# Sparse-attention scores over 128 contraction rows, shared keys projected feature-major, compression with two stacked parts

## The chip, the core and the metric

The kernel runs on one core of a Trainium2 chip. The core has five engines with an instruction queue each: TensorE (PE in the profile; its weight loads are listed as PEld), VectorE (DVE), ScalarE (ACT), GpSimd (POOL) and SyncE (SP), which here only issues weight loads from HBM. Products go from SBUF through PE into PSUM banks of 128 partitions by 512 float32, and ACT and DVE read them from there. The metric is the device time of one execution in microseconds (us), from the start of the program to its end; lower is better.

## The reference

Two transformer blocks on 256 tokens of width 1024, all in float32. The first block (gated mix of three attentions, feed-forward) is not touched. The second has two layers: feed-forward, a spatial gating unit, feed-forward; then feed-forward, a native sparse attention (NSA), feed-forward. Keys and values of the sparse attention are made from the activations that enter the second layer (`kv`, six slots of 4 groups by 64 features):

```python
kv = (h @ kv_w).reshape(B, S, N_KV_SLOTS, N_KV_GROUPS, HEAD_DIM_2)
k_cmp = compress(kv[:, :, 0], cmp_pe[0], cmp_w1[0], cmp_b1[0], cmp_w2[0])
v_cmp = compress(kv[:, :, 1], cmp_pe[1], cmp_w1[1], cmp_b1[1], cmp_w2[1])
# slots 2, 3: keys and values of the selected blocks; slots 4, 5: of the window
...
def compress(kv, pe, w1, b1, w2):      # 15 blocks of 32 tokens, stride 16, per group
    ...
    return jax.nn.gelu(flat @ w1 + b1, approximate=False) @ w2      # flat: 2048 wide, w1: 2048 x 256
```

With 256 tokens every selected block lies inside the causal range, so selection and window both come down to causal attention of 16 heads over all earlier tokens, once with the keys of slot 2 and values of slot 3, once with slots 4 and 5, with a bias by distance; the compressed branch adds attention over the 15 compressed keys and values.

## The kernel before, in words

**Precision.** PE multiplies float32 exactly only in four slow passes. So most operands are kept as two float32r parts, high and low (`wh`, `wl` of a weight; two `big` tiles of activations), and a product is three matmuls: high by high, high by low, low by high (`mm3`, L273 to L275). In the profile such a matmul shows as L273, L274 or L275, whoever called it. `up` (weights stationary, all 256 tokens moving, output feature-major, two tiles of 128 features by 256 tokens in a bank) takes 48 matmuls of 256 columns per chunk of weights; `row` (activations stationary, weights moving, output token-major) takes 24 matmuls per 128 tokens, of as many columns as the weights have.

**Weights.** `Stream` loads them in the order of use, in half chunks of 512 KB (5 raw buffers `wr`), splits each with a cast on ACT (L140) and a subtraction on DVE (L147), and holds four chunks of split weights. Every `W.get` takes the next chunk and prepares those that follow.

**The stage that is changed, `kv_ffn` (L985).** It runs the projection of `kv` ahead of the first feed-forward of the second layer and hides its small work in that feed-forward: the generator `ff` loops over chunks `c` of 256 hidden features (two `up`, the activation, then the product into the accumulators, `down`, L309) and calls `hooks[c]` on the way.
- The projection is token-major: three chunks of 512 columns, each for two tiles of 128 tokens (`row`, 24 matmuls of 512 columns). ACT copies the results from PSUM into `kvc` (slots 0 and 1, L996), `ks` (keys, L998) and `self.v` (values, L999).
- `heads_T` (L1019) turns a slot feature-major: DVE duplicates each group's 64 features side by side (L1024), PE transposes (8 per slot, L1029), so each group lies on both halves of the partitions. The hook `keys` (c = 1) does so for slots 2 and 4 and splits them into `self.kh` and `self.kl`; the hooks `windows(0)` and `windows(1)` (c = 2, 3) do so for slots 0 and 1, one half shifted by a token (L1059 on ACT, L1060 on DVE), add the position term (L1070) and split the result.
- The hook `compress` (c = 4, L1074) multiplies, for each of two slots, 60 blocks (15 by 4 groups) by `w1` in 16 steps of 128 rows with `mm3`: 48 matmuls with 60 stationary columns and 256 moving ones. DVE copies the result (L1085), PE transposes it in two pieces (L1089, 60 rows), ACT applies the gelu (L1091), and products with `w2` follow (L1097; L1112 after eight DVE copies, L1106).

**The scores, in `nsa` (L1123).** `stack` puts the queries of a head into `Q` with the high part on one half of the partitions and the low part on the other. For each of 4 heads, 4 groups and 2 token tiles `score` writes a bank with two matmuls: `Q[:, j]` by `kh` over all 128 rows (L1273: high and low query by the high key), then the high half `Q[a, j]` by the same half of `kl` (L1274: 64 rows). Both move `2 * nk` columns: 256 for the first token tile, 512 for the second. `attention` (L635) runs groups of heads in a pipeline: scores two groups ahead of the transposes (L667), those one ahead of the products with the values (L681); DVE adds the mask and takes the minimum (L657), ACT applies exp (L659).

**What sets the order.** A list scheduler of the tile framework orders each engine's instructions when the kernel is built; each engine then runs its own list strictly in order, and semaphores hold it where an operand or buffer is not ready. Weight loads stand in the order of `Stream`.

## Time and profile before

| what | value |
|---|---|
| three runs, median (lowest to highest) | 1521.57 us (1514.3 to 1526.19) |
| span of the profiled execution, first to last instruction | 1511.4 us |
| PE busy | 1469.7 us, 97% of the span, 9817 matmuls |
| DVE busy | 955.1 us, 63% |
| ACT busy | 745.9 us, 49% |
| POOL busy | 64.9 us, 4% |
| granted TensorE clock, mean | 0.995 |
| read from HBM | 262.09 MB, 174 GB/s over the span |

The span lies 10.2 us under the median and 2.9 us under the fastest of the three runs; what lies around the first and last instruction is in the runs' times and not in the span. Matmuls are pipelined, so the length of one in the profile (0.28 us for 256 columns, 0.39 us for 512) is not what it costs a busy PE: that is the distance from its start to the start of the next, called a slot here.

### The profile page before, as it was taken

What the parts mean: (1) busy time and instruction counts of PE and PEld (TensorE: products, weight loads), DVE (VectorE), ACT (ScalarE), POOL (GpSimd) and SP (SyncE); (2) the same over time, 40 slices, a digit from 0 to 9 for tenths busy, and PEclk for the clock granted to TensorE, in tenths of its full rate; (3) what the DMA queues carried; (4) which work ended last, traced back from release to release, by engine and by line L of the source; (5) the groups of instructions that cost most, each with busy time, mean ns of one, the idle gap of its engine ahead of it and who ended that gap; (6) DMA issues with size and microseconds to landing.
All of it is one profiled execution on the core that took longest, in us unless ns stands there. A gap on an engine that the chain in (4) does not pass through costs nothing.

```text
span 1511.4 us, 24692 instructions
## 1 busy us (share of the span) xinstructions
PE 1469.7 (97%) x9817; PEld 1323.7 (88%) x9817; DVE 955.1 (63%) x1611; ACT 745.9 (49%) x1141; POOL 64.9 (4%) x79
## 2 busy tenths in 40 slices
PE   7999999999999999999999999999999999999997
PEld 6798987989889999799889999799999787899996
DVE  7884388555584555876774455767655777765545
ACT  5565554444454443544454443545544486444442
POOL 0000030000000000100010000100000121100002
PEclk9999999999999999999999999999999999999999
DMA  8352266655646556576556655555765442275550
GB/s 283 116 181 88 77 232 223 210 184 185 190 168 189 186 184 194 171 206 245 173 173 190 191 185 182 168 176 188 255 186 182 145 141 65 70 242 189 184 181 28
DMA packets 188640, 264.78 MB, mean 175 GB/s; under 512 B 11024, under 2 KB 153708, under 8 KB 188524
## 3 DMA queue, kind: packets, MB, share of 16 engines
q1 hardware_dynamic: 179996, 249.56, 51.5%
q10 hardware_dynamic: 8528, 13.64, 3.0%
q8 instruction: 77, 1.26, 0.3%
q14 instruction: 39, 0.32, 0.1%
HBM read 262.09 MB, written 1.07 MB: 174 GB/s over the span
## 4 chain that ended last, share of the span: by engine, by line
PE 76%; DVE 6%; DMA 1%; ACT 1%; issue 0%; POOL 0%; DVEq 0%; ACTq 0%; SPq 0%
PE acc L309 21%; PE u L273 15%; PE u L275 15%; PE u L274 15%; DVE big L836 1%; PE acc L681 1%; PE acc L273 1%; PE acc L275 1%; PE acc L274 1%; DVE bst L366 1%; DVE big L813 1%; PE u L1274 1%; PE acc L667 1%; DMA wr<-in_ffn_w_dram 1%; DVE nwa L335 1%; DMA wr<-in_w_mlp_out_dram 1%
## 5 line engine op out<-in xcount | busy, mean ns | idle before, releaser
L147 DVE TENSOR_TENSOR wl<-wr,wh 128x1024 fp32r<-128x1024 f32 (+4 forms) x488 | 577.1, 1191 | 447.0 <-ACT wh L140 443.2
L140 ACT CAST wh<-wr 128x1024 fp32r<-128x1024 f32 (+4 forms) x488 | 494.2, 1019 | 545.1 <-PE u L274 240.2
L273 PE MATMUL u<-big,wh 128*128 128x256 f32 x1896 | 534.1, 282 | 1.1 <-ACT med L399 0.9
L275 PE MATMUL u<-big,wl 128*128 128x256 f32 x1896 | 532.0, 281 | 0.0
L274 PE MATMUL u<-big,wh 128*128 128x256 f32 x1896 | 531.9, 281 | 0.0
L273 PEld LDWEIGHTS u<-big,wh 128*128 128x128 f32 x1896 | 356.9, 188 | 4.7 <-ACT med L399 1.1
L274 PEld LDWEIGHTS u<-big,wh 128*128 128x128 f32 x1896 | 356.4, 188 | 2.5
L275 PEld LDWEIGHTS u<-big,wl 128*128 128x128 f32 x1896 | 356.8, 188 | 0.0
L309 PE MATMUL acc<-wh,t 128*128 128x512 f32 x928 | 263.5, 395 | 1.4 <-ACT t L322 1.2
L309 PEld LDWEIGHTS acc<-wh,t 128*128 128x128 f32 x928 | 170.1, 188 | 37.0 <-ACT t L322 1.4
L309 PE MATMUL acc<-wl,t 128*128 128x512 f32 x464 | 145.3, 394 | 0.0
L273 PE MATMUL u<-wh,big 128*128 128x512 f32 (+2 forms) x352 | 120.6, 343 | 1.5 <-DVE big L323 1.0
L275 PE MATMUL u<-wh,big 128*128 128x512 f32 (+2 forms) x352 | 119.4, 339 | 0.0
L274 PE MATMUL u<-wl,big 128*128 128x512 f32 (+2 forms) x352 | 119.0, 338 | 0.0
L309 PEld LDWEIGHTS acc<-wl,t 128*128 128x128 f32 x464 | 87.0, 188 | 20.5 <-DVE wl L147 0.4
L822 POOL TENSOR_TENSOR big<-big,med 128x256 f32<-128x256 f32 x46 | 33.6, 764 | 1176.8 <-ACT big L821 1140.8
L273 PEld LDWEIGHTS u<-wh,big 128*128 128x128 f32 (+1 forms) x352 | 64.3, 183 | 11.7 <-DVE big L323 2.6
L322 ACT CAST t<-t 128x512 fp32r<-128x512 f32 x66 | 41.0, 621 | 67.3 <-DVE t L522 23.5
L275 PEld LDWEIGHTS u<-wh,big 128*128 128x128 f32 (+1 forms) x352 | 64.3, 183 | 7.5
L274 PEld LDWEIGHTS u<-wl,big 128*128 128x128 f32 (+1 forms) x352 | 64.3, 183 | 7.3
L323 DVE TENSOR_TENSOR t<-t,t 128x512 fp32r<-128x512 f32 x66 | 45.3, 686 | 15.4 <-ACT t L322 15.2
L273 PE MATMUL acc<-wh,t 128*128 128x512 f32 x112 | 45.4, 410 | 2.7 <-ACT t L322 2.7
(252 smaller groups left out, 1298.6 us busy)
## 6 DMA issues: line engine op xcount, KB each, us to landing
wr<-in_ffn_w_dram SPq DMA_DIRECT2D x264, 512.0 KB, 4.0
wr<-in_w_in_dram SPq DMA_DIRECT2D x34, 512.0 KB, 4.6
wr<-in_w_mlp_in_dram SPq DMA_DIRECT2D x32, 512.0 KB, 4.0
wr<-in_w_mlp_out_dram SPq DMA_DIRECT2D x32, 512.0 KB, 4.3
wr<-in_sgu_w_in_dram SPq DMA_DIRECT2D x32, 512.0 KB, 6.2
wr<-in_sgu_w_out_dram SPq DMA_DIRECT2D x16, 512.0 KB, 4.5
wr<-in_kv_w_dram SPq DMA_DIRECT2D x12, 512.0 KB, 3.8
wr<-in_w_out_dram SPq DMA_DIRECT2D x8, 512.0 KB, 6.3
```

Of the source, the lines that this page charges most:

```text
L140: self.nc.scalar.copy(h, v)
L147: self.nc.vector.tensor_sub(l, v, h.bitcast(F32))
L273: mm(out, lh, rh, start=start, stop=False, **k)
L274: mm(out, lh, rl, start=False, stop=False, **k)
L275: mm(out, ll, rh, start=False, stop=stop, **k)
L309: mm(acc[t][n], a[:, k, ts], b[:, 0, n * 512:(n + 1) * 512], start=s, stop=e)
L322: self.nc.scalar.copy(h, x)
L323: return self.nc.vector.tensor_sub(l, x, h.bitcast(F32))
L335: nc.vector.tensor_scalar(a, y, y, nh, op0=OP.mult, op1=OP.mult)
L366: b = nc.vector.bn_stats(st[:, 6 * i:6 * i + 6], x[:, c0:c1])
L667: nc.tensor.transpose(pt[:, c:c + 128], e[:, c:c + 128], self.ident)
L822: nc.gpsimd.tensor_mul(x[:, cs], x[:, cs], gB[:, cs])
```

## The change

Four edits in the second block, beside docstrings and comments that are dropped (which moves line numbers).

1. **Keys feature-major.** The chunks of `kv_w` are cut by slot (1024 rows by 256 columns) where they were cut in 512 columns. The value slots 3 and 5 stay token-major, side by side in a bank, with 256 moving columns. Slots 0, 1, 2 and 4 go through `up`, which gives them feature-major with two groups in a tile of 128 features. `heads_T`, its DVE copies and its transposes go. For the keys each group is copied from its half of the partitions to both halves of `kh` (ACT), and the low part is made for both halves of `kl` (DVE); for slots 0 and 1 ACT copies one half and DVE the shifted other.
2. **Compression in two products.** High and low part of the blocks lie side by side: columns 0 to 59 high, 60 to 63 zero, 64 to 123 low. A matmul with 124 stationary columns by the high weights gives high by high and low by high on separate output rows, one with 60 columns by the low weights adds the rest. The two row blocks are added by the product that transposed: the moving operand `two` is the identity written twice, one above the other (124 rows).
3. **Scores.** The second matmul takes all 128 rows of `Q` and `kl`.
4. The build reserves less scratch for software DMA descriptors.

```diff
 def kv_ffn(self, x, acc):
...
-        def row(ws, j, t):
...
-        for j in range(1, 3):
-            ws = ld(j)
-            for t in range(2):
-                row(ws, j, t)
+        def ld(slot, pump=True):
+            return W.get(kvw, 0, KT, slot * 256, (slot + 1) * 256, pump)
+
+        ws = [ld(3)]
         yield
+        ws.append(ld(5, False))
         for t in range(2):
+            ps = self.bank()
+            for b in range(2):
+                self.row(ws[b], *x, ps[:, b * 256:(b + 1) * 256], t)
+            nc.scalar.copy(self.v[:, :, t], ps.rearrange("p (b d) -> p b d", b=2))
             yield
         W.pump()
+        def key(b):
+            w = ld(2 + 2 * b)
+            ps = self.bank()
+            self.up(w, *x, ps)
+            for a in range(2):
+                p = ps[:, a * S:(a + 1) * S]
+                for e in range(2):
+                    g = 2 * a + e
+                    for d in range(2):
+                        h = self.kh[half[d], g, b]
+                        nc.scalar.copy(h, p[half[e]])
+                    q = self.kh[half[e], g, b].bitcast(F32)
+                    for d in range(2):
+                        nc.vector.tensor_sub(self.kl[half[d], g, b], p[half[e]], q)
+        def tokens(slot):
+            w = ld(slot)
+            ps = self.bank()
+            self.up(w, *x, ps)
+            T = self.med([128, 4, S])
+            for a in range(2):
+                p = ps[:, a * S:(a + 1) * S]
+                for e in range(2):
+                    nc.scalar.copy(T[:64, 2 * a + e], p[half[e]])
+                    nc.vector.tensor_copy(T[64:, 2 * a + e, :S - 1], p[half[e], 1:])
+            Ts.append(T)
+        for slot in range(2):
+            tokens(slot)
+        for b in range(2):
+            key(b)
...
-        def heads_T(slot, put):
...
 def compress():
...
-                        self.mm3(ps[:60, :256], fl[0][:, s, k], fl[1][:, s, k], wh[:, i], wl[:, i], k == 0, k == 15)
+                        f = fl[s][:, k]
+                        ops = [(124, wh), (60, wl)]
+                        for m, w in ops[::-1] if k == 15 else ops:
+                            nc.tensor.matmul(ps[:m, :256], f[:, :m], w[:, i], start=k == 0 and m == 124,
+                                             stop=k == 15 and m == 124, skip_group_check=True)
...
-                nc.vector.tensor_copy(r[:60], ps[:60, :256])
+                nc.vector.tensor_copy(r[:124], ps[:124, :256])
...
-                    nc.tensor.transpose(ps[:, f * 60:(f + 1) * 60], r[:60, f * 128:(f + 1) * 128], self.ident[:60, :60])
+                    nc.tensor.matmul(ps[:, f * 60:(f + 1) * 60], r[:124, f * 128:(f + 1) * 128], self.two[:124, :60],
+                                     start=True, stop=True)
...
 def score(ps, t=t, g=g, h=h, nk=nk, nxt=nxt):
...
-                    nc.tensor.matmul(o, Q[a, j], self.kl[a, g, :, :nk], start=False, stop=True)
+                    nc.tensor.matmul(o, Q[:, j], self.kl[:, g, :, :nk], start=False, stop=True)
...
-    nc = bacc.Bacc("TRN2", target_bir_lowering=False, num_devices=1)
+    nc = bacc.Bacc("TRN2", target_bir_lowering=False, num_devices=1, dynamic_dma_scratch_size=1024)
```

The scheduler's order on PE, between the last compression product of the first slot and the first of the second (`u` a bank, `wh_`/`wl_` split weights, `t_` a scratch tile, `cst` the identity; sizes are output rows by columns), before:

```order
L274 MATMUL u<-wl_76,big 60x256
L275 MATMUL u<-wh_75,big 60x256
L309 MATMUL acc<-wh_2000,t_9694 128x512 x2
L309 MATMUL acc<-wl_2001,t_9694 128x512 x2
L309 MATMUL acc<-wh_2000,t_9695 128x512 x2
L1089 MATMUL u<-cst,t_9929 128x60 x2
L273 MATMUL u<-wh_77,big 60x256
```

and now:

```order
L1087 MATMUL u<-wl_76,big 60x256 x2
L1087 MATMUL u<-wh_75,big 124x256
L309 MATMUL acc<-wh_2000,t_9828 128x512 x3
L309 MATMUL acc<-wl_2001,t_9828 128x512 x2
L1095 MATMUL u<-two,t_10030 128x60 x2
L1087 MATMUL u<-wh_77,big 124x256
L1087 MATMUL u<-wl_78,big 60x256
```

Five accumulator products stand between the last compression product and the one that waits for its copy, where there were six; the compression products alternate between 124 and 60 output rows.

The same after the second slot, before:

```order
L275 MATMUL u<-wh_71,big 60x256
L309 MATMUL acc<-wh_2002,t_9694 128x512 x2
L309 MATMUL acc<-wl_2003,t_9694 128x512 x2
L309 MATMUL acc<-wh_2002,t_9695 128x512 x2
L1089 MATMUL u<-cst,t_9998 128x60 x2
L1097 MATMUL u<-hid_9932,w2d 128x60 x2
L309 MATMUL acc<-wh_2000,t_9694 128x512 x2
L309 MATMUL acc<-wl_2001,t_9694 128x512 x2
L309 MATMUL acc<-wh_2000,t_9695 128x512 x2
L309 MATMUL acc<-wh_2002,t_9694 128x512
L1112 MATMUL u<-w_9372,med 128x64
```

and now:

```order
L1087 MATMUL u<-wh_71,big 124x256
L309 MATMUL acc<-wh_2000,t_9829 128x512 x2
L309 MATMUL acc<-wh_2002,t_9828 128x512 x2
L1095 MATMUL u<-two,t_10083 128x60 x2
L1104 MATMUL u<-hid_10033,w2d 128x60 x2
L309 MATMUL acc<-wl_2003,t_9828 128x512 x2
L309 MATMUL acc<-wh_2002,t_9829 128x512 x2
L309 MATMUL acc<-wh_2000,t_9828 128x512
L309 MATMUL acc<-wl_2001,t_9828 128x512
L1119 MATMUL u<-w_9521,med 128x64
```

Four accumulator products stand ahead of the waiting product where there were six, and six ahead of the first product with the copies of the gelu's output (L1112, now L1119) where there were seven.

On ACT, where the last projections are read out of PSUM and the first activation of the feed-forward follows (L521), before:

```order
L998 COPY med<-u 128x256
L999 COPY v<-u 128x256
L1042 DMA med<-in_cmp_pe_dram 32x128
L140 CAST wh_73<-wr_68 128x1024
L140 CAST wh_75<-wr_64 128x1024
L140 CAST wh_77<-wr_65 128x1024
L998 COPY med<-u 128x256
L999 COPY v<-u 128x256
L140 CAST wh_79<-wr_66 128x1024
L521 ACTIVATE t_9197<-u 128x256
```

and now:

```order
L1033 COPY med<-u 64x256
L140 CAST wh_75<-wr_64 128x1024
L1017 CAST big<-u 64x256 x4
L140 CAST wh_77<-wr_65 128x1024
L1017 CAST big<-u 64x256 x2
L140 CAST wh_79<-wr_66 128x1024
L1017 CAST big<-u 64x256 x6
L521 ACTIVATE t_9381<-u 128x256
L1017 CAST big<-u 64x256 x2
L140 CAST wh_69<-wr_67 128x1024
```

The key copies of 64 partitions stand between the casts of the weights, and most of them ahead of the first activation; the casts keep their distance to the chunk that PE works on.

## Rows read from the trace of the kernel before

**Rows 1.** The page: span, busy time by engine

```profile
span 1511.4 us, 24692 instructions
...
PE 1469.7 (97%) x9817; PEld 1323.7 (88%) x9817; DVE 955.1 (63%) x1611; ACT 745.9 (49%) x1141; POOL 64.9 (4%) x79
```

**Rows 2.** Busy time by stretch: kv projection, then four stretches of scores

```profile
core 0: us, PE busy (x) PEld busy (x) DVE busy (x) ACT busy (x) POOL busy (x), PEclk, DMA share, GB/s
958.00:986.00 28.00, 28.00 (x123) 22.62 (x122) 19.47 (x22) 14.66 (x20) 0.00 (x0) 1.00 0.72 237
...
1216.00:1228.00 12.00, 12.00 (x79) 9.77 (x78) 10.35 (x42) 11.13 (x41) 3.52 (x4) 1.00 0.59 194
1228.00:1250.00 22.00, 22.00 (x153) 17.98 (x152) 16.18 (x58) 15.15 (x47) 2.97 (x4) 1.00 0.22 64
1250.00:1262.00 12.00, 12.00 (x84) 9.95 (x83) 8.55 (x45) 8.97 (x35) 3.03 (x4) 1.00 0.00 1
1262.00:1284.00 22.00, 20.81 (x139) 16.34 (x139) 15.76 (x55) 13.89 (x47) 2.09 (x3) 1.00 0.31 96
```

**Rows 3.** Timeline of PE, kv projection: start us, us, weights as rows*columns

```profile
960.73 0.39 PE L273 MATMUL u<-wh,big 128*128 128x512 f32 x1
...
962.36 0.40 PE L274 MATMUL u<-wl,big 128*128 128x512 f32 x1
```

**Rows 4.** Timeline of PE, the eight transposes of one slot

```profile
1028.21 1.04 PE L1029 MATMUL u<-cst,med 128*128 128x128 f32 x8
1029.00 0.72 PE L309 MATMUL acc<-wh,t 128*128 128x512 f32 x2
```

**Rows 5.** Timeline of PE, into and out of the first slot's 48 compression products

```profile
1063.53 0.28 PE L275 MATMUL u<-big,wl 128*128 128x256 f32 x1
1063.65 0.28 PE L273 MATMUL u<-wh,big 128*60 128x256 f32 x1
...
1069.17 0.28 PE L275 MATMUL u<-wh,big 128*60 128x256 f32 x1
1069.29 0.64 PE L309 MATMUL acc<-wh,t 128*128 128x512 f32 x2
...
1070.87 0.33 PE L1089 MATMUL u<-cst,t 60*128 60x60 f32 x2
```

**Rows 6.** Timeline of PE, behind the second slot

```profile
1078.32 0.33 PE L1089 MATMUL u<-cst,t 60*128 60x60 f32 x2
...
1080.75 0.33 PE L1112 MATMUL u<-w,med 128*128 128x64 f32 x2
```

**Rows 7.** Timeline of PE, score pairs of 512 columns, one pair behind the other

```profile
1275.05 0.50 PE L1273 MATMUL u<-big,t 128*128 128x512 f32 x1
...
1275.90 0.49 PE L1273 MATMUL u<-big,t 128*128 128x512 f32 x1
```

**Rows 8.** Timeline of PE, a score pair with transposes behind it

```profile
1229.07 0.39 PE L1273 MATMUL u<-big,t 128*128 128x512 f32 x1
...
1229.82 0.66 PE L667 MATMUL acc<-cst,t 128*128 128x128 f32 x4
```

**Rows 9.** Timeline of PE, two score pairs of 256 columns among other 256-column products

```profile
1219.41 0.28 PE L275 MATMUL u<-big,wl 128*128 128x256 f32 x1
1219.52 0.28 PE L1273 MATMUL u<-big,t 128*128 128x256 f32 x1
1219.73 0.38 PE L1274 MATMUL u<-big,t 64*128 64x256 f32 x1
...
1220.89 0.28 PE L274 MATMUL u<-big,wh 128*128 128x256 f32 x1
```

**Rows 10.** DVE groups by line and shape, 940 to 1110 us: busy, mean ns

```profile
L147 DVE TENSOR_TENSOR wl<-wr,wh 128x1024 fp32r<-128x1024 f32 x60 | 72.7, 1221 | 44.4 <-ACT wh L140 44.0
...
L323 DVE TENSOR_TENSOR big<-u,big 128x256 fp32r<-128x256 f32 x8 | 3.1, 403 | 0.3 <-ACT big L322 0.3
```

**Rows 11.** An ACT group by line and shape, same stretch and columns

```profile
L999 ACT COPY v<-u 128x256 f32<-128x256 f32 x4 | 1.5, 379 | 0.0
```

More of the change, by code (lines that the diff above doesn't have):

```diff
@@ L1004, in kv_ffn @@
-        ws = W.get(kvw, 0, 4, 0, 512)
-        yield
-        ws = ws + W.get(kvw, 512, 4, 0, 512, False)
-        for t in range(2):
-            row(ws, 0, t)
+        self.kh, self.kl = (self.big([128, 4, 2, S], F32R) for _ in range(2))
+        half = [slice(0, 64), slice(64, 128)]
+        def ld(slot, pump=True):
+            return W.get(kvw, 0, KT, slot * 256, (slot + 1) * 256, pump)
+        ws = [ld(3)]
+        yield
+        ws.append(ld(5, False))
+        for t in range(2):
+            ps = self.bank()
+            for b in range(2):
+                self.row(ws[b], *x, ps[:, b * 256:(b + 1) * 256], t)
+            nc.scalar.copy(self.v[:, :, t], ps.rearrange("p (b d) -> p b d", b=2))
@@ L1009, in kv_ffn @@
             yield
         W.pump()
-        for j in range(1, 3):
-            ws = ld(j)
-            for t in range(2):
-                row(ws, j, t)
-        self.kh, self.kl = (self.big([128, 4, 2, S], F32R) for _ in range(2))
+        def key(b):
[12 more added lines that the diff above has]
+                        nc.vector.tensor_sub(self.kl[half[d], g, b], p[half[e]], q)
@@ new lines, in kv_ffn @@
+        Ts = []
+        def tokens(slot):
[11 more added lines that the diff above has]
+            tokens(slot)
@@ L1016, in kv_ffn @@
+        for b in range(2):
+            key(b)
         fl = []
         pe = self.p2.tile([128, 2, 16], F32, name="pe")
-        def heads_T(slot, put):
-            d = self.med([128, 2, 4, 2, 64])
-            for t in range(2):
-                src = kvc[:, t, slot * 256:(slot + 1) * 256] if slot < 2 else ks[:, slot // 2 - 1, t]
-                src = src.rearrange("p (g d) -> p g d", g=4)
-                nc.vector.tensor_copy(d[:, t], src[:, :, None, :].to_broadcast([128, 4, 2, 64]))
-            for a in range(2):
-                ps = self.bank()
-                for g in range(2):
-                    for t in range(2):
-                        nc.tensor.transpose(ps[:, g * S + t * 128:g * S + (t + 1) * 128],
-                                            d[:, t, 2 * a + g].rearrange("p a b -> p (a b)"), self.ident)
-                put(a, ps.rearrange("p (g s) -> p g s", g=2))
@@ L1033, in keys @@
-        def keys():
-            for slot in (2, 4):
-                def put(a, ps):
-                    o = (slice(None), slice(2 * a, 2 * a + 2), slot // 2 - 1)
-                    self.split(self.kh[o], self.kl[o], ps)
-                heads_T(slot, put)
-                per = self.med([32, 128])
+        def keys():
+            per = self.med([32, 128])
             nc.scalar.dma_start(per, I["cmp_pe_2"].rearrange("s (j a) d -> (s j) (a d)", a=2))
@@ L1051, in keys @@
                 nc.scalar.dma_start(self.w2d[:, :, i], I["cmp_w2_2"][0].rearrange("(f p) d -> p f d", p=128))
-            fl.extend(self.big([128, 2, 16, 60], F32R) for _ in range(2))
+            fl.append(self.big([128, 16, 128], F32R))
+            fl.append(self.big([128, 16, 128], F32R))
+            self.two = self.p2.tile([128, 64], F32, name="two")
+            nc.vector.tensor_add(self.two, self.ident[:, :64], self.ident[:, 64:])
         def windows(slot):
-            T = self.med([128, 4, S])
-            def put(a, ps):
-                gs = slice(2 * a, 2 * a + 2)
-                nc.scalar.copy(T[:64, gs], ps[:64])
-                nc.vector.tensor_copy(T[64:, gs, :S - 1], ps[64:, :, 1:])
-            heads_T(slot, put)
+            T = Ts[slot]
             flt = self.med([128, 16, 4, 15])
@@ L1070, in windows @@
             nc.vector.tensor_add(flt, src, pes)
-            self.split(fl[0][:, slot], fl[1][:, slot], flt.rearrange("p j g n -> p j (g n)"))
+            f = flt.rearrange("p j g n -> p j (g n)")
+            nc.vector.memset(fl[slot][:, :, 60:64].bitcast(F32), 0.0)
+            self.split(fl[slot][:, :, :60], fl[slot][:, :, 64:124], f)
         def compress():
@@ L1269, in score @@
                         stack(*nxt)
-                    a, j = hb(h), 2 * (h % 2) + h // 2
+                    j = 2 * (h % 2) + h // 2
                     Q = qs[t, g]
```

10 lines of the change are left out of this document (removed).

## The prediction

> **What bounds the kernel now.** I read the page first: PE is busy for 1469.7 of 1511.4 us, DVE for 63% and ACT for 49% [rows 1]. So the kernel is a queue of matmuls, and a change is worth what it takes out of PE's queue, less what PE then waits. Next the busy time by stretch, for the places that the change touches [rows 2]: in the kv projection and in the first three stretches of scores PE has no idle time at all, in the last one 1.2 us. There is little waiting to win back; each term is matmuls times their slot (start to next start). The columns for DVE and ACT show how much room each has if PE gets faster: much in the projection (19.5 and 14.7 of 28 us), little in the first stretch of scores (10.35 and 11.13 of 12 us).
>
> **1. Projection: 0.** Before: 3 chunks x 2 token tiles x 24 = 144 matmuls of 512 columns. Seven slots take 1.63 us [rows 3], 0.233 each, in all 33.6 us. After: 96 token-major and 192 feature-major ones of 256 columns. 47 slots of 256 columns take 1069.17 - 1063.65 = 5.52 us [rows 5], 0.117 each, in all 33.8 us. Twice the matmuls at half the slot: no change. The copies out of PSUM grow in number, to 24 of 64 x 256 on each of ACT and DVE. The nearest rows have as many elements per partition: 0.379 us on ACT [rows 11], 0.403 on DVE [rows 10]. A key chunk then asks 8 x 0.40 + 2 x 1.22 (the weights' low parts) = 5.6 us of DVE, just what PE takes for its 48 matmuls, a chunk of slot 0 or 1 4.1 us. What hides a lag is that split weights lie up to four chunks ahead, and the order keeps them there. I take 0. No row copies from one half of the partitions to the other, as half of these do: from below nothing is gained, from above twice the time, 24 x 0.4 = 9.7 us more of DVE in a stretch in which DVE now idles 8.5 us; I allow 1.5 us of that to reach PE.
>
> **2. Transposes of the four slots: -3.2.** Eight take 0.79 us [rows 4], 32 take 3.2 us. They stand between saturated products, so all of it is won. Their DVE duplication goes too, under cover.
>
> **3. Compression: -3.8, and +1.0 of waits.** 96 matmuls become 64: 32 x 0.117 = 3.8 us. Columns don't count: into and out of 60 stationary columns the slots are 0.12 us [rows 5]. But what follows is a chain through DVE and ACT, and its cover shrinks. From the first slot's last product to the transposes that need DVE's copy it takes 1.70 us [rows 5], of which six accumulator products and a slot fill 1.52. It waits 0.2 now; for the second slot, with the same six products, I take the same. With five in their place 1.28 us are filled and PE waits 0.4 us, with four behind the second slot 1.05 us and 0.6 to 0.7: 0.6 more together, less some 0.2 for the changes to and from 60 rows that end with these transposes (priced under 4): +0.4. From the second slot's transposes to the product that needs the gelu and eight DVE copies it takes 2.43 us [rows 6]; now four small products of 0.11 and six of 0.233 fill 1.84: +0.6. Who stands behind these waits is the feed-forward's next `up`, that is all of PE. If the copy falls behind a 1.22 us weight subtraction on DVE [rows 10], each wait can grow by that: bound +3.
>
> **4. Scores: -11.4 of matmuls, of which 9.0 reach the end.** A 64-row product costs much more than its columns. Two neighbouring 512-column starts of the same line lie 0.85 us apart [rows 7]; two plain slots are 0.466: 0.385 us per pair are lost. Between 256-column products two pairs and the product behind take 1219.52 to 1220.89 = 1.37 us where five plain slots would take 0.57 [rows 9]: 0.40 per pair. The slot ahead of the 64 rows grows (0.21 for 0.11), its own is 0.31, the next one grows too. With transposes behind, the pair takes 0.75 us [rows 8], 0.28 over plain, and 0.05 more show in the transposes. The timeline has 32 pairs: 13 with a float32r product behind, 19 with a transpose or value product. That gives 13 x 0.39 + 19 x 0.33 = 11.4 us; the loss sits at the change between 128 and 64 rows, and after the change there is none.
>
> The Trainium skill says so too, on its page TensorEngine Tiling, section Tiling Modes (Key Properties): changing the tiling mode, and not merely the tile, drains TensorE. The trace agrees for rows (0.31 for 0.117). By its section Performance Considerations a contraction of 64 or less is, however, where row tiling pays, which speaks against filling 128 rows; here a 64-row product stands alone between 128-row ones, and its slot is 0.31 and not half of 0.117, so nothing of that is given up.
>
> Not all of it reaches the end. The scores of the first token tile, 256 columns each, lie at 1216 to 1228 and 1250 to 1262 us, eight pairs in each. Without 8 x 0.36 us PE has 9.1 us of work there, while ACT has 11.13 and 8.97 us and DVE 10.35 and 8.55 [rows 2]. The pipeline is two groups deep and ACT can catch up in the stretches behind (15.15 of 19.2 us), so I take half of the first stretch's excess, 1.0 us, and 0.7 in the other stretch where all three engines would be near 9. In the last stretch PE's lead over DVE and ACT shrinks by the 2 us that five pairs in a row give up; I take 0.7. So 11.4 - 2.4 = 9.0. Bounds: 11.4 if all lag is absorbed; 6 if PE waits for ACT throughout both short stretches and the last lead is lost.
>
> **The rest: 0.** Smaller scratch and the earlier loads of later constants move no instruction on PE's path. Weight loads keep order, size and number.
>
> **Sum.** 0 - 3.2 - 3.8 + 1.0 - 9.0 = -15.0 us. Of the profiled span that leaves 1496.4 us. I apply the same difference to the median, since the 10.2 us between span and median lie outside what is changed: 1521.57 - 15.0 = **1506.6 us**, 0.99% less. The runs of before spread over 12 us, so about 1% is what a measurement of this kernel can tell from no change; the forecast stands just at that line.
>
> **Rivals.**
> - *ACT and DVE become the bound of the scores.* For it: 11.13 of 12 us on ACT. Against: they wait for PE later, 15.15 of 22. The scores then give 4 to 6 us and not 9: 1510 to 1512 us. It decides once the lag of the first stretch is not made up.
> - *The row change is not the cause*, and the slots stay at 0.31 and 0.43 with 128 rows, say because both products load the same queries as weights. Against: the pattern of long slots begins and ends with the 64 rows [rows 9]. Then term 4 is 0: 1515.7 us.
> - *Changing the number of stationary columns drains PE as well.* Some 60 changes between 124 and 60 at the 0.2 us of a row change would cost 12 us and leave 1518.6 us, within 1%. Against: 0.12 us into and out of 60 columns [rows 5]. The Trainium skill's page TensorEngine Tiling, section Tiling Modes, lists 64-column arrays as modes of their own, so by its rule on draining this would happen; the trace doesn't show it.
> - *Slower: the copies between the halves of the partitions.* If each of the 24 DVE operations takes p instead of 0.40 us, DVE sets the pace of the projection. The loss is at most 24 x (p - 0.40); it eats the whole gain at p = 1.02 us and gives a slower kernel above, at p = 1.6 by 14 us (1536 us). For it: no row prices such a copy. Against: every copy of 256 elements per partition takes about 0.4 us, and four prepared chunks must first be used up.
>
> - *The waits don't come*: ACT's and DVE's lag is absorbed everywhere and the order covers the chains. For it: PE has next to no idle time anywhere in these stretches now [rows 2]. The gain is 3.2 + 3.8 + 11.4 less at most 1: 1503 to 1504.5 us.
>
> **How the numbers follow.** The forecast with its own bounds (scores 8 to 10, waits 0.5 to 2) covers 1505 to 1509 us and has 0.42; no waits 0.22; ACT and DVE as bound 0.22; row change not the cause 0.05; columns drain 0.05; slower 0.04. Leaving out the last three, and with some 3.5 us of scatter of a median added on either side, the range is 1499 to 1515 us. Faster by over 1% means below 1506.4: the case without waits and half of the forecast, 0.43, and I put 0.44. Within 1% are the other half, the bound by ACT and DVE and the two rivals of PE: 0.52. Slower: 0.04.
>
> **What would show it.** In the profile after: the second score product at 128*128 with slots of 0.233 and 0.117; compression slots of 0.117 alternating 124 and 60 columns; no transposes in the hooks; PE's idle time, now near none, up by 2 to 4 us, ahead of the two products with `two`, of L1119 and in 1216 to 1262. The prediction is wrong if the projection's stretch gets longer, if the compression slots exceed 0.13 us, or if PE idles more than 5 us among the scores.

## The result, and the profile after

The changed kernel takes 1500.86 us (median of 4 runs, 1499.05 to 1502.52) beside 1523.88 us (4 runs) of the kernel before: a ratio of 0.9855, with an interval of 0.9813 to 0.9898. Taken again, it took 1498.77 us beside 1518.73 us of the kernel before, 0.9834 (0.9787 to 0.9882). It is faster by about 1.5%, some 20 us, where 15 us were forecast. The profiled execution of before, on which the sum was made, spans 1511.4 us and that of after 1500.0 us. Between these two profiles the difference is thus only 11.4 us, and one question of this study is why the medians lie further apart than the profiles.

The page after, which answers [rows 1]: PE has 14.6 us less to do, and it now takes 84 more matmuls for it.

```profile
span 1500.0 us, 24889 instructions
...
PE 1455.1 (97%) x9901; PEld 1325.4 (88%) x9901; DVE 956.6 (64%) x1622; ACT 746.8 (50%) x1149; POOL 64.1 (4%) x79
```

The busy time by stretch in after, which answers [rows 2]. In this trace the projection lies about 1 us later than before, the start of the scores 2 us and their end 11 us earlier, and the stretches are moved to match.

```profile
core 0: us, PE busy (x) PEld busy (x) DVE busy (x) ACT busy (x) POOL busy (x), PEclk, DMA share, GB/s
960.00:988.00 28.00, 28.00 (x240) 28.00 (x239) 22.82 (x31) 15.95 (x25) 0.00 (x0) 1.00 0.80 253
1214.00:1225.00 11.00, 10.81 (x91) 10.30 (x90) 10.83 (x43) 10.90 (x40) 2.97 (x4) 1.00 0.72 222
1225.00:1245.00 20.00, 20.00 (x159) 18.66 (x158) 16.93 (x65) 15.81 (x49) 3.09 (x4) 1.00 0.21 63
1245.00:1257.00 12.00, 11.77 (x97) 11.18 (x97) 11.00 (x48) 10.87 (x45) 3.08 (x4) 1.00 0.08 33
1257.00:1275.00 18.00, 16.05 (x117) 13.83 (x116) 13.65 (x48) 12.24 (x38) 1.86 (x2) 1.00 0.30 97
```

The projection (first row) has PE busy throughout, as before. Among the scores PE now has small gaps, and in the first stretch DVE and ACT are busy for 10.83 and 10.90 of 11 us.

The timeline of PE in after at two score pairs of 256 columns, the place of [rows 9]; columns are the start, the duration, and the weights as rows*columns:

```profile
1216.77 0.28 PE L275 MATMUL u<-big,wl 128*128 128x256 f32 x1
1216.88 0.28 PE L1280 MATMUL u<-big,t 128*128 128x256 f32 x1
1216.99 0.28 PE L1281 MATMUL u<-big,t 128*128 128x256 f32 x1
1217.11 0.28 PE L1280 MATMUL u<-big,t 128*128 128x256 f32 x1
1217.22 0.28 PE L1281 MATMUL u<-big,t 128*128 128x256 f32 x1
1217.34 0.28 PE L273 MATMUL u<-big,wh 128*128 128x256 f32 x1
1217.45 0.28 PE L274 MATMUL u<-big,wh 128*128 128x256 f32 x1
```

From the product ahead of the pairs to the second one behind them it takes 1217.45 - 1216.77 = 0.68 us, six plain slots; the same six took 1220.89 - 1219.41 = 1.48 us before [rows 9]. Two 512-column pairs in a row, the place of [rows 7], start 0.47 us apart where it was 0.85:

```profile
1264.88 0.39 PE L1280 MATMUL u<-big,t 128*128 128x512 f32 x1
...
1265.35 0.39 PE L1280 MATMUL u<-big,t 128*128 128x512 f32 x1
```

The compression in after, which answers [rows 5, 6]: the first slot's products, the stacked copy's products (L1095), and the wait behind the second slot.

```profile
1063.21 0.28 PE L1087 MATMUL u<-wh,big 128*124 128x256 f32 x1
1063.33 0.28 PE L1087 MATMUL u<-wl,big 128*60 128x256 f32 x1
...
1066.86 0.28 PE L1087 MATMUL u<-wh,big 128*124 128x256 f32 x1
...
1068.36 0.55 PE L1095 MATMUL u<-two,t 124*128 124x60 f32 x4
...
1073.52 0.62 PE L1095 MATMUL u<-two,t 124*128 124x60 f32 x4
...
1076.81 0.43 PE L1119 MATMUL u<-w,med 128*128 128x64 f32 x2 [0.76 <-DVE med L1113]
```

31 slots take 1066.86 - 1063.21 = 3.65 us, 0.118 each, with 124 and 60 columns in turn.

What PE waited for in after between 985 and 1085 us (total, times, longest):

```profile
PE u L482 <- DVE t L522: 1.3, 1, 1.3
PE u L1119 <- DVE med L1113: 0.8, 1, 0.8
```

The products of L482 transpose the feed-forward's first activations, those of L1119 are the last ones of the compression. Neither wait stood in the kernel before; in a second trace of the changed kernel the first is 1.4 us and the second doesn't stand. Between 1205 and 1290 us PE waits 1.9 us at L710 for DVE's output rows (1.2 us before) and twice 0.2 us for the queries.

**Where the time went.** PE's instructions of two traces can be matched one to one. The table gives by how much the difference of their starts (kernel minus before's trace) moved in two stretches: the projection with feed-forward and compression (from the median over 940 to 985 us to that over 1090 to 1180 us of before's time), and the queries with the scores (from 1200 to 1215 us to 1290 to 1300 us). "Clock" is what a lower granted clock behind the scores took away, 10 us x (1 - granted clock), summed over the 10 us windows from 1270 to 1300 us.

| kernel | projection, compression | scores | of it clock |
|---|---|---|---|
| changed, two traces | -4.1, -4.5 | -8.9, -9.3 | 0, 0 |
| key projection alone | -1.4 | +4.9 | 5.1 |
| compression alone | -3.4 | 0.0 | 0 |
| score product alone | 0.0 | -9.3 | 0 |
| changed, 64-row score product | -4.4 | +4.9 | 5.2 |
| changed, keys first | -5.7 | -9.3 | 0 |
| before, two more traces | 0.0, 0.0 | +3.3, +6.5 | 3.4, 6.8 |

So the changed kernel gains 13 to 14 us by stages, 4 of them in the first stretch and 9 in the scores. Up to 940 us the other traces lie between 2.7 us ahead of before's and 5.0 us behind it, two traces of the changed kernel at -2.7 and +1.2, so that part has nothing to do with the change. The first trace of the changed kernel lost these 1.2 us and another 0.6 us just ahead of the scores; so 13.0 us by stages are 11.4 us between the spans. The column on the clock shows something that was not in the sum: in four traces of this table with the 64-row product the clock fell behind the scores.

### The profile page after: what moved, and what is told of

Its sections match the earlier page's. It is cut to its first block, busy times and chain, and to the rows that moved or that the text cites. A ratio compares the mean times of both kernels' runs of the same rounds, so it can differ in the third digit from the quotient of the medians.

```text
span 1500.0 us, 24889 instructions
## 1 busy us (share of the span) xinstructions
PE 1455.1 (97%) x9901; PEld 1325.4 (88%) x9901; DVE 956.6 (64%) x1622; ACT 746.8 (50%) x1149; POOL 64.1 (4%) x79
## 4 chain that ended last, share of the span: by engine, by line
PE 83%; DVE 9%; DMA 3%; ACT 3%; issue 1%; POOL 0%; DVEq 0%; ACTq 0%; SPq 0%; POOLq 0%
PE acc L309 21%; PE u L273 18%; PE u L274 17%; PE u L275 17%; DVE wl L147 2%; PE acc L681 2%; DVE big L836 1%; PE acc L273 1%; PE acc L274 1%; PE acc L275 1%; ACT wh L140 1%; DVE bst L366 1%; PE acc L667 1%; DVE big L813 1%; DMA wr<-in_w_out_dram 1%
## 5 line engine op out<-in xcount | busy, mean ns | idle before, releaser
L273 PE MATMUL u<-big,wh 128*128 128x256 f32 x1960 | 553.3, 282 | 1.0 <-ACT med L399 0.9
L274 PE MATMUL u<-big,wh 128*128 128x256 f32 x1960 | 551.3, 281 | 0.0
L275 PE MATMUL u<-big,wl 128*128 128x256 f32 x1960 | 551.2, 281 | 0.0
L273 PEld LDWEIGHTS u<-big,wh 128*128 128x128 f32 x1960 | 370.2, 189 | 4.5 <-ACT med L399 1.1
L274 PEld LDWEIGHTS u<-big,wh 128*128 128x128 f32 x1960 | 369.7, 189 | 2.4
L275 PEld LDWEIGHTS u<-big,wl 128*128 128x128 f32 x1960 | 370.1, 189 | 0.0
L273 PE MATMUL u<-wh,big 128*128 128x256 f32 (+1 forms) x304 | 103.2, 339 | 1.3 <-DVE big L323 0.8
L274 PE MATMUL u<-wl,big 128*128 128x256 f32 (+1 forms) x304 | 101.2, 333 | 0.0
L275 PE MATMUL u<-wh,big 128*128 128x256 f32 (+1 forms) x304 | 101.2, 333 | 0.0
L273 PEld LDWEIGHTS u<-wh,big 128*128 128x128 f32 x304 | 57.8, 190 | 9.6 <-DVE big L323 2.5
L275 PEld LDWEIGHTS u<-wh,big 128*128 128x128 f32 x304 | 57.9, 190 | 5.8
L274 PEld LDWEIGHTS u<-wl,big 128*128 128x128 f32 x304 | 58.0, 191 | 5.3
```

Of the source, the lines that this page charges most:

```text
L273: mm(out, lh, rh, start=start, stop=False, **k)
L274: mm(out, lh, rl, start=False, stop=False, **k)
L275: mm(out, ll, rh, start=False, stop=stop, **k)
```

## The experiments

**The kernel before, again (two runs).** No edit.

> The kernel before, unchanged. Its runs so far lie between 1514.3 and 1528.1 us, and its profiled execution (1511.4 us of span) is the shortest of them. Theory 1: the scatter is between executions of one program, so this copy gives 1514 to 1528 us, a ratio of 1.00, and its profile will show where 7 to 14 us can go without a change in the program: a stretch in which TensorE is granted less than 1.0, or a wait for a transfer. Theory 2: the profiled execution was a lucky one, and most lie at 1522 to 1528 us; then the change is worth about 23 us in the medians but 11 us between profiles, and the other 10 us lie in a stretch that the change does not touch.

> The kernel before once more, for another trace. Half of its runs so far lie at a mean granted clock under 0.992, down to 0.982, and no trace so far is of a run under 0.991: the falls behind the scores seen in traces are worth 3 to 5 us, the slowest runs 20 us. Theory (the fall begins where the scores' 64-row products end and lasts longer in the slow runs): a stretch of clock under 1.00 that begins between 1270 and 1290 us and is longer the lower the run's mean. Rival (another stretch carries it): a long fall elsewhere, as in the first attention near 150 us or around 250 us, with 1.00 from 1260 to 1320 us.

The first copy gives 1516.2 to 1530.6 us in ten runs, a ratio of 0.9991 (0.9956 to 1.0027), and the kernel before, run beside it, 1510.1 to 1533.9 us. Theory 1 holds, and of theory 2 the first half: the profiled execution of before belongs to the shortest. (The highest of the ten runs lies 2.6 us above the range that theory 1 named.) Over the 65 runs of before that stand beside the experiments, time and mean granted clock go together with a correlation of -0.98: 0.001 less of clock is 1.46 us more. 43 of the 65 lie under 0.993. The 18 runs at 0.994 or more have a median of 1514.2 us, all 65 one of 1520.6 us. The second copy's trace shows the place; windows of 10 us, PE alone, with the granted clock behind the count:

```profile
core 0: us, PE busy (x), PEclk, DMA share, GB/s
1270.00:1280.00 10.00, 8.81 (x49) 1.00 0.35 125
1280.00:1290.00 10.00, 10.00 (x50) 0.52 0.03 9
1290.00:1300.00 10.00, 10.00 (x55) 0.80 0.01 2
```

Of these 20 us from 1280 us on the clock is at its lower level, 1.2 GHz, for 2 x (4.8 + 2.0) = 13.6 us, and 6.8 us are lost. Ahead of that PE had gone through the 32 pairs with their 64-row products, so the stretch is one that the change does touch. The second half of theory 2 falls for the larger part: of the 8.6 us by which the second copy's trace is longer than before's, 6.5 lie there, and in the first copy, where the window from 1280 us has 0.66, 3.3 of 6.8; most of what is left lies ahead of 940 us. In before's own trace, the one of [rows 1], the window has 1.00. Of what was expected of the second copy, the place of the fall came; that the fall is longer the lower the run's mean clock is not shown, for both copies were profiled at a mean of 0.991. In the same windows of after:

```profile
1260.00:1270.00 10.00, 8.05 (x56) 1.00 0.31 109
1270.00:1280.00 10.00, 10.00 (x75) 1.00 0.00 0
```

PE idles longer at the end of the scores than before, 1.95 of 10 us in place of 1.19, and the clock stays. The idle time does not tell the two kernels apart here. The Trainium skill's page TensorE: Matmul & The Clock Gate, section HAM oscillation — how this bites in real kernels, names idle gaps of TensorE as what throttles it; no trace of this case shows that behind the scores, where the longer gaps go with the steady clock. It agrees with the end of the executions, where PE has no work left: in after's window from 1490 to 1500 us PE is busy for 0.03 us and the granted clock is 0.75.

**The score product alone.**

```diff
-nc.tensor.matmul(o, Q[a, j], self.kl[a, g, :, :nk], start=False, stop=True)
+nc.tensor.matmul(o, Q[:, j], self.kl[:, g, :, :nk], start=False, stop=True)
```

> The kernel before with the second score product over 128 rows instead of 64; nothing else of the change. Theory (a change of the rows between the two products of a pair drains TensorE, and most of what it costs reaches the end): second products at 0.233 us a slot in place of 0.4 to 0.6, the scores stretch 9 us shorter, 1505 to 1507 us beside 1515.7 us, or 9 us below whatever the kernel before gives in the same rounds. Rival 1 (ScalarE and VectorE become the bound of the scores): 4 to 6 us shorter, with TensorE idle for over 5 us among the scores. Rival 2 (the rows are not the cause): the slots keep their length and the time stays.

1505.8 us (1502.8 to 1508.5, 4 runs), a ratio of 0.9876 (0.9808 to 0.9943), clock 0.995 or 0.996 in every run. The scores' stretch is 9.3 us shorter. The theory holds, rivals 1 and 2 fall. In the medians it brings 15 us rather than 9: of the kernel before, run beside it, 19 of 25 runs lie under a clock of 0.993, and of this kernel none.

**The changed kernel with the 64-row product.** The diff above, undone.

> The changed kernel with its second score product put back to 64 rows; the key projection and the compression stay changed. Theory: 9 us slower than the changed kernel, so 4 to 6 us below the kernel before by profiles. If the key projection feature-major also helps the scores by itself (another layout, other buffers), it stays nearer to the changed kernel; if the gain in the medians (23 us) comes from elsewhere, it stays some 10 us or more below the kernel before.

1513.1 us (1507.4 to 1527.2, 10 runs), 0.9939 (0.9901 to 0.9977); the clock goes from 0.984 to 0.996 again. At 0.994 or more the three runs have a median of 1509.1 us, 8 to 9 us above the changed kernel, as the theory has it; all ten have one 12 us above it. So both the gain and the steady clock hang on this one product.

**The key projection alone.** The diff of the change's function `kv_ffn` without the stacked compression.

> The kernel before with the feature-major projection of the shared keys alone (its copies included); compression and scores as before. Theory: the eight transposes of 0.4 us each go (3.2 us less), and the wait of the first feed-forward transposes for a chain of small copies between ScalarE and VectorE, 1.3 us in the trace after, comes: 1.5 to 2 us less than before in the compared profiles, a ratio of 0.9985 to 1.000. Rival: the copies cost as much as the transposes saved, no difference in the stretch from 945 to 1010 us; other rival: this part carries the 10 us by which the medians differ more than the profiles.

1517.7 us (10 runs), 0.9987 (0.9954 to 1.002); -1.4 us in its stretch, with the wait at L482 of 1.5 us. The theory holds, just under the 1.5 to 2 us that it named: 3.2 us of transposes, less 1.5 us. Both rivals fall.

**The compression alone.** Upper and lower parts side by side in 124 columns, the two products with the stacked identity, and the smaller scratch of edit 4.

> The kernel before with the stacked compression alone. Theory: 48 slots of 0.117 us go and 48 of 0.117 us stay short of their changes of columns, and the two products with the stacked identity cost a wait of about 1 us: 2.8 us less than before in the stretch of the compression, 0.8 us of wait at L1119 of the changed kernel included. The clock scatters as in the kernel before, since its scores are unchanged, so the trace decides and not the median. Rival (124 and 60 columns in turn drain TensorE): slots over 0.13 us and no gain.

1517.5 us (10 runs), 0.9985 (0.9948 to 1.0022); -3.4 us in its stretch. It gains 0.6 us more than expected, and the wait at L1119 does not come in this trace. The rival falls with the slots of 0.118.

**The keys ahead of the tokens.** An attempt to do better than the changed kernel.

```diff
-        for slot in range(2):
-            tokens(slot)
         for b in range(2):
             key(b)
+        for slot in range(2):
+            tokens(slot)
```

> The changed kernel, unchanged, beside the next three. So far the kernels whose second score product has 64 rows scatter over 15 to 24 us with their mean granted clock (0.982 to 0.997), and the two with 128 rows over 4 to 6 us (0.994 to 0.997). Theory (the 64-row products bring on a stretch of lower clock behind the scores in most executions): 1498 to 1504 us again, clock 0.994 or more in every run, 1.00 between 1270 and 1290 us. Rival (four runs were too few to see it): some runs at 1508 us or more with a clock under 0.992.

> The changed kernel with the two shared-key chunks projected and copied before the two token chunks, so that the copies between ScalarE and VectorE don't stand ahead of the first feed-forward activation. Theory: the wait of the transposes L482 for VectorE (1.3 us) goes, 1 to 1.5 us below the changed kernel beside it. Rival: another set of copies (the tokens' eight) takes that place, or the weight preparation behind them is late: no difference, or up to 1 us longer.

The changed kernel gives 1496.3 to 1502.0 us at a clock of 0.994 or more in all four runs: the clock as expected, two of the times below the range. The wait at L482 is 1.4 us in its trace, and with the keys first it is gone; one small wait stands in this stretch:

```profile
PE u L1119 <- DVE med L1113: 0.2, 1, 0.2
```

The stretch gains 1.2 us more than in the changed kernel beside it (-5.7 for -4.5). In the time this is not to be seen: 1498.66 us (1496.9 to 1500.0, 4 runs) beside 1498.77. The cause of the wait is shown, a faster kernel is not.

**Two score products in the other order.** Before, with the products of every odd head swapped; the 64-row products of two neighbouring heads, which lie on different halves of the rows and write different banks, come to stand side by side.

```diff
+if h % 2:
+    nc.tensor.matmul(o, Q[a, j], self.kl[a, g, :, :nk], start=True, stop=False)
+    nc.tensor.matmul(o, Q[:, j], self.kh[:, g, :, :nk], start=False, stop=True)
+else:
     nc.tensor.matmul(o, Q[:, j], self.kh[:, g, :, :nk], start=True, stop=False)
     nc.tensor.matmul(o, Q[a, j], self.kl[a, g, :, :nk], start=False, stop=True)
```

> The kernel before with the two score products of every odd head in the other order, so that the rows run 128, 64, 64, 128, 128, 64, 64 instead of 128, 64, 128, 64: half as many changes of the number of rows, the same products. Theory 1 (each change costs about as much as the other): about half of the 11.4 us of slots goes, 4 to 6 us less than before at the same granted clock. Theory 2 (a 64-row product is slow in itself, or the loss comes from the transposes and value products between them): no difference. For the clock, theory A (rows that stand idle in the array bring the fall behind the scores) expects the scatter of before (0.983 to 0.997) here too; theory B (the drains do) expects it halved.

1512.3 us (10 runs), 0.9935 (0.9904 to 0.9966); -4.2 us in the scores. Theory 1 holds for the time. In its timeline of PE the two 64-row products start at the same time:

```profile
1221.16 0.28 PE L275 MATMUL u<-big,wl 128*128 128x256 f32 x1
1221.27 0.28 PE L1277 MATMUL u<-big,t 128*128 128x256 f32 x1
1221.48 0.38 PE L1278 MATMUL u<-big,t 64*128 64x256 f32 x1
1221.48 0.38 PE L1274 MATMUL u<-big,t 64*128 64x256 f32 x1
1221.79 0.38 PE L1275 MATMUL u<-big,t 128*128 128x256 f32 x1
1222.01 0.28 PE L273 MATMUL u<-big,wh 128*128 128x256 f32 x1
1222.12 0.28 PE L274 MATMUL u<-big,wh 128*128 128x256 f32 x1
```

The six products take 1222.12 - 1221.16 = 0.96 us. Two of them share a slot, so five plain slots are 0.57 us, and 0.39 us are left for two changes of rows. The clock lies under 0.993 in three of ten runs, where before, run beside it, has 11 of 19. Theory A expected the scatter of before, theory B half of it; ten runs can't tell these apart.

**Both score products over 64 rows.**

```diff
-nc.tensor.matmul(o, Q[:, j], self.kh[:, g, :, :nk], start=True, stop=False)
+nc.tensor.matmul(o, Q[a, j], self.kh[a, g, :, :nk], start=True, stop=False)
```

> The kernel before with both score products of a head over its 64 rows; what is left out is the product of the queries' lower parts with the keys' upper parts, so the scores are a little less exact. No change of rows within a pair, and as many columns as before. Theory 1 (the change of rows costs, not the rows): both products at 0.233 us or less a slot in pairs with nothing between, 5 to 9 us less than before at the same granted clock; where the transposes (128 rows) stand between them, a change remains. Theory 2 (a 64-row product costs more in itself): the slots stay at those of before or grow. For the clock, theory A (idle rows) expects a lower clock behind the scores at least as often as before, 0.983 to 0.996 over the runs; theory B (drains) expects 0.994 or more.

1511.3 us (10 runs), 0.9948 (0.991 to 0.9987). The scores gain 2.2 us in a trace whose clock lost 3.4 us behind them (0.66 from 1270 to 1280 us), so 5.6 us at an even clock: theory 1. The timeline of PE; x2 is two products in one row:

```profile
1219.08 0.28 PE L275 MATMUL u<-big,wl 128*128 128x256 f32 x1
1219.29 0.38 PE L1273 MATMUL u<-big,t 64*128 64x256 f32 x2
1219.51 0.28 PE L1274 MATMUL u<-big,t 64*128 64x256 f32 x2
1219.72 0.39 PE L273 MATMUL u<-big,wh 128*128 128x256 f32 x1
1219.94 0.28 PE L274 MATMUL u<-big,wh 128*128 128x256 f32 x1
```

Six products take 0.86 us. Four of them, on two halves, go in two slots, so four plain slots are 0.45 us, and again 0.41 us are left for two changes. Before, with four changes, the same count gives 1.48 - 0.68 = 0.80 us. Three kernels agree on 0.20 us for one change of rows.

Where these 0.20 us lie shows in the weight loads. Before, the load for the 128-row product starts at 1219.41 us, one slot ahead of its product (1219.52), and is covered; the load for the 64-row product starts only with its own product, at 1219.73 [rows 9]:

```profile
1219.41 0.19 PEld L1273 LDWEIGHTS u<-big,t 128*128 128x128 f32 x1
1219.73 0.18 PEld L1274 LDWEIGHTS u<-big,t 64*128 64x128 f32 x1
```

In after the load for the second product of a pair starts one slot ahead too (the product stands at 1216.99):

```profile
1216.88 0.19 PEld L1281 LDWEIGHTS u<-big,t 128*128 128x128 f32 x1
```

So at a change of rows the load of 0.18 or 0.19 us is not covered, which is about the size of the cost. Whether the load is the cause, or only starts late because the engine empties first, no run here separates.

For the clock, three of ten runs are under 0.993, down to 0.985. That is against theory B, which expected 0.994 or more; theory A expected falls at least as often as before (11 of 19 runs beside it), and that isn't shown either.

**A 64-row edge, and the same edge over 128 rows.** Before, with the second score product cut behind all but 16 keys of each half; `r` is `a` (64 rows) in one kernel and all 128 rows in the other.

```diff
-nc.tensor.matmul(o, Q[a, j], self.kl[a, g, :, :nk], start=False, stop=True)
+e = nk - 16
+nc.tensor.matmul(o[:, :, :e], Q[:, j], self.kl[:, g, :, :e], start=False, stop=False)
+nc.tensor.matmul(o[:, :, e:], Q[r, j], self.kl[r, g, :, e:nk], start=False, stop=True)
```

> The kernel before with the second score product cut in two along its columns: all but 16 keys of each half over 128 rows, the last 16 keys of each half (32 columns) over 64 rows. So each of the 32 pairs has the two changes of rows of the kernel before, but its array is half idle for 32 columns only. Theory of the change of rows: slots of the scores about as long as before or up to 2 us longer (a third small product in each pair), 1512 to 1516 us at a clock of 0.996. Rival (64-row columns are slow in themselves): near the kernel with 128 rows throughout, 1504 to 1506 us. For the clock, theory A (idle rows bring the fall behind the scores): 0.994 or more in every run; theory B (the drains at the changes bring it): 0.983 to 0.996, in about half of the runs under 0.993, as before.

> The same cut of the second score product, the last 32 columns over 128 rows like the rest: no change of rows, but the same third product in each pair. Theory: each third product costs its own slot of some 0.06 us or the weight load ahead of it (0.19 us) where nothing covers that: 1505 to 1508 us at a clock of 0.996, 6 to 9 us below the kernel with the 64-row edge, and a clock of 0.994 or more in every run under both theories of the clock. Rival (the third product itself costs what the change of rows seems to): as long as the kernel with the 64-row edge.

1515.4 us (1514.2 to 1517.0, 10 runs) for the 64-row edge, 1508.3 us (1505.9 to 1511.5, 6 runs) for the other; in the scores +0.4 and -7.1 us against before. Groups by line and shape, the first row of the 64-row edge, the second of the 128-row edge (busy, mean ns of one | idle before):

```profile
L1276 PE MATMUL u<-big,t 64*128 64x32 f32 x32 | 9.0, 280 | 0.0
```

```profile
L1276 PE MATMUL u<-big,t 128*128 128x32 f32 x32 | 5.8, 183 | 0.0
```

Products of only 32 columns cost the kernel 0.4 + 7.1 = 7.5 us if they take 64 rows, not far from the 9.3 us that the 256 or 512 columns of before cost. It is the change of rows, not the number of columns under it. Two pairs of the 64-row edge from the timeline of PE:

```profile
1220.73 0.28 PE L1273 MATMUL u<-big,t 128*128 128x256 f32 x1
...
1222.10 0.28 PE L274 MATMUL u<-big,wh 128*128 128x256 f32 x1
```

They and the product behind take 1222.10 - 1220.73 = 1.37 us, as long as the two pairs and the product behind before [rows 9], and have the same number of columns and of changes. And the clock: with the edge all 64 changes are there and the array is half idle for 32 columns only, and no run of ten is under 0.993 (one lies at 0.993, where theory A expected 0.994 or more), while of before beside it 13 of 21 are. So the changes of rows alone do not bring the clock down. What is left are the long products over 64 rows. Whether it is the rows that stand idle in them (theory A) is not shown: in the two kernels before this, pairs of them run at the same time on both halves, and three of ten runs of each lie under 0.993 all the same. The 128-row edge missed its expectation, 0.994 or more, in two of six runs (0.992 and 0.993). Of the 105 runs with the long 64-row products as in before, in four kernels, 66 lie under 0.993; of the 16 with two products over 128 rows (the changed kernel twice, the score product alone, keys first) none; of the 128-row edge one of six.

## Why the prediction was right, and where it was off

- **The reading of the bound** held. PE is busy 97% in both kernels, and what came out of its queue came out of the time.
- **Term 1, projection 0**: held in its place, PE 28.00 of 28.00 us in the projection. The copies between the halves cost 0.367 us on ACT and 0.422 us on DVE (groups by line, 16 of 64x256 each), near the 0.38 and 0.40 taken from [rows 10, 11]; the slower rival needed over 1.02 us. But the 1.5 us that were "allowed" came, elsewhere: what was covered were the split weights, and what was late were the feed-forward's first activations, which stand behind the key copies in the queues of ACT and DVE. ACT and DVE do these copies by turns, each waiting for the other (the bracket names who was waited for, and for how long):

```profile
989.93 1.50 ACT L1017 CAST big<-u 64x256 fp32r<-64x256 f32 x4
993.37 0.75 ACT L1017 CAST big<-u 64x256 fp32r<-64x256 f32 x2 [1.93 <-DVE big L1020]
994.14 0.39 ACT L521 ACTIVATE t<-u 128x256 f32<-128x256 f32 x1
994.15 0.87 DVE L1020 TENSOR_TENSOR big<-u,big 64x256 fp32r<-64x256 f32 x2 [0.82 <-ACT big L1017]
995.05 0.74 ACT L1017 CAST big<-u 64x256 fp32r<-64x256 f32 x2 [0.52 <-DVE big L1020]
```

The sentence "What hides a lag is that split weights lie up to four chunks ahead" left out the work queued behind the copies. PE then waits 1.3 to 1.5 us at L482. The copies were priced by their sum on each engine, and the chain across the two engines was not.
- **Term 2, transposes -3.2**: held; alone -1.4 us with the 1.5 us wait in it.
- **Term 3, compression -3.8 + 1.0**: alone -3.4 us; together with the other parts a wait of 0.8 us at L1119 in one trace of two. The slots of the matmul term held (0.118 us); of the waits, the one at L1119 comes in that trace only, and PE's waits name none ahead of the products with `two` in either. The rival on columns falls: 0.118 us between 124 and 60 columns.
- **Term 4, scores -11.4, of which 9.0 reach the end**: 8.9 to 9.3 us in three kernels. Its parts were each too large. PE's idle time among the scores grew from 1.2 to 2.3 us, 1.1 us more where 2.4 was taken; so the slots gave some 10.1 us, not 11.4. One reason can be read: of the four distances between 512-column pairs in a row, priced at 0.47 us, one is that; the others are 0.54, 0.54 and 0.66 us. The two errors cancel, which is luck. The 0.7 us for the last stretch came as forecast, at L710 (1.9 us for 1.2); of the 1.7 us for the two short stretches 0.4 came in this trace. ACT and DVE do come near the bound in the first stretch (10.90 and 10.83 of 11 us), but PE idles 0.19 us there.
- **The sum** of -15.0 us: by stages -13.0 and -13.8, in runs at a clock of 0.994 or more 1514.2 to 1500.3 us (18 and 8 runs), -13.9. Most of the missing 1 to 2 us is the wait at L482, for which the sum had no term.
- **The step from the profile to the median failed.** "I apply the same difference to the median, since the 10.2 us between span and median lie outside what is changed" was wrong. About 3 us of it lie outside the span (1514.3 for 1511.4 in that execution); the other 7 were time that the profiled execution didn't lose, a lower clock, and part of it falls behind the very products that the change removes. The medians differ by 1520.6 - 1500.3 = 20 us: 14 of slots, and 6 that the clock gave back. So the forecast of 1506.6 us was 6 us too high. The result lies in the stated range, 1.9 us above its lower end, and that is in part luck: that end was set by the case in which no waits come and by 3.5 us of scatter, and neither is what happened. The sum had no term for the clock. Of the outcomes, the one that came, faster by over 1%, had been given 0.44, less than the 0.52 for within 1%.

What stays open: the clock's falls in traces cost 3.4 to 6.8 us, in five of the eight traces with long 64-row products (two of the three of before, the key projection alone, the 64-row score product in the changed kernel, both products over 64 rows). Ahead of the scores every trace, with 64 rows or 128, loses another 2 to 7 us to the lower clock (windows of 10 us). The slowest runs of before, at 0.982 and 0.983, are nearly 20 us above the fastest, and no profile fell on one of them. Where the rest of theirs lies isn't shown. Nor is it shown why one execution falls and the next doesn't.

## What to carry to other kernels

A product over 64 rows between products over 128 cost two changes of 0.20 us in the kernels here, with 512 columns as with 32: give it all 128 rows, with the other half doing something useful or harmless, or put short-row products of different halves and banks side by side. When small copies are moved to another place, price the chain across the engines that do them, and look at what stands behind them in each queue; a sum per engine hides both. And when runs of a kernel scatter by more than its profiled execution explains, look at the granted clock of each run before a difference of profiles is applied to the median: the profile may be of the execution that escaped.

## What the runs showed of the hardware that was not expected

- Long products over 64 rows were followed, in five of eight traces, by 7 to 14 us of the lower clock level; with 128 rows, and with 64 rows on 32 columns only, in none of six. Idle time of TensorE does not sort these traces: the wait of 1.2 us at L710 stands in traces with the fall (the key projection alone) and without (before, the compression alone), and the 1.9 us of after bring none.
- Two 64-row products on different halves of the rows, into different banks, run at the same time: both start at 1221.48 us, and four take two slots. The prediction saw the 64-row product "stand alone" and had no row for this. The Trainium skill's page TensorEngine Tiling (Array Packing), section Tiling Modes (Key Properties), says that tiles operate independently, and that a change of mode drains the engine; the traces agree with the first, and with the second in that a change of rows costs, 0.20 us. Even the kernel with 64 rows throughout, which leaves a product out, needs two slots and two changes for two heads, 0.23 + 0.40 = 0.63 us, where four slots over 128 rows take 0.47 us.
- A change of the stationary columns (124, 60, 128) costs nothing that the slots show, 0.118 us throughout.
